# Chunk attention with its weight remainders on VectorE instead of GpSimd

## The chip, the core and the metric

The kernel runs on one core of a Trainium2 chip. The metric is the device time of one execution in microseconds (us); smaller is better. The engines are TensorE (PE, with PEld for its weight loads), VectorE (DVE), ScalarE (ACT), GpSimd (POOL) and SyncE (SP), whose queue issues almost all transfers. Each engine works through its own instructions in the order of the program, and instructions of different engines wait for each other through semaphores.

## The reference

A two-layer trunk over 512 frames of width 1024. Layer 0 is a state-space mixer beside a convolution module; layer 1 is the chunk attention that the change touches; each layer is followed by cross-attention into 256 memory tokens. Layer 1, cut to what matters (chunks of 64 frames, each of which sees itself and the 8 before it; 16 heads of 64):

```
q, k, v, g = jnp.split(h @ w_in, 4, axis=-1)          # h: 512 x 1024, w_in: 1024 x 4096
s = einsum('bqhd,bkhd->bhqk', qc, kc) * scale + bias  # for each chunk, bias by clipped distance
s = where(valid, s, -1e30)
o = einsum('bhqk,bkhd->bqhd', softmax(s), vc)
x = x + (o * silu(g)) @ w_out
```

All products are wanted in near float32 precision.

## The kernel before

**Products in three parts.** Every large matrix product splits both operands into a rounded part (`hi`) and a remainder (`lo`), and sums hi·hi, hi·lo and lo·hi. Activations are split once. A block of weights, 128 x 8 x 128 or 128 x 4 x 256 (1024 numbers per partition), is loaded by SyncE into `raw`, rounded by a ScalarE cast into `whi`, and its remainder `raw - whi` goes into `wlo`. That is `weights`, which calls `split`; the engine of the subtraction is the argument `eng`, and GpSimd where none is given. There are three buffers of `raw`, two of `whi` and three of `wlo`.

**Units as filler.** In chunk attention the 32 weight blocks of queries, keys, gates (24 blocks, `qk_unit`, `g_unit` and `first`) and values (8 blocks, `v_unit`) are worked off by generators that yield after each matmul. The products that need `wlo` stand last in each unit: 16 of 24 matmuls come before them. The class `Filler` hands out so many matmuls between the steps of the attention as the lists `GAPS`, `LEAST` and so on allow; TensorE's order is therefore written out in full and pinned.

**Eight pairs of heads.** The loop over `hp` treats two heads at a time; the text calls them pair 0 to pair 7. For each pair the scores are made in three goes, rows 0 and 1, row 2, and row 3 (a row is 128 queries; row i has 128 (i+1) keys). Behind each go VectorE finds the peak with the bias (`peak`, L1269 to L1272), ScalarE takes the exponential (L1257), VectorE the reciprocal and the scaling (L1259, L1260, recorded as L162: tiles `pe0` to `pe3`, in the profile `pe`). Then TensorE transposes the scaled rows (L84, `transposed`) with filler between, VectorE and ScalarE split each transposed block (`pt`), and the weighting by the values follows in the next pair. The last transpose of the first block needs the scaled row 3 of the first head, `pe` 128x512.

In the same stretch VectorE and ScalarE finish queries and keys (`qk_finish`: `z`, then casts and subtractions, half of these on GpSimd by the table `QE`), gates, values, and the output of the pair before (`output`: two additions into `o`, the gating L157 `o<-o,g`, the cast to `og` on ScalarE and the remainder of `og` on GpSimd). `tz` is a head's bias table, loaded and shifted once for each head (L1235, recorded as L162).

A list scheduler sets the order of VectorE's and ScalarE's instructions by its own estimates; `tc.high_priority()` puts a group ahead of others. Helpers record under their own lines: L153 is `tt`, L157 is `stt`, L162 is `ts` with one operand, L168 the cast in `split`.

Of the kernel before, what the change touches and what calls it, by code (L numbers as in the profile page):

```python
# [18 lines left out]
SEQ = 512  # L19
MEM = 256  # L20
# [24 lines left out]
def kernel(  # L45
# [22 lines left out]
    V, A, G = nc.vector, nc.scalar, nc.gpsimd  # L68
# [43 lines left out]
    def tl(tag, shape=(P, SEQ), dt=F32):  # L112
        pool, n = tags[tag]
        return pool.tile(list(shape), dt, tag=tag, name=nm(tag), bufs=n)

    def rl(tag, shape=(P, SEQ)):
        return tl(tag, shape, F32R)
# [10 lines left out]
    def psum(tag):  # L128
        return pp.tile([P, 512], F32, tag=tag, name=nm("ps_" + tag), bufs=PS[tag])
# [16 lines left out]
    def f(ap):  # L146
        return ap.bitcast(F32)

    def pinned(ins):
        tc.keep_in_program_order(ins)  # L150

    def tt(out, a, b, op, eng=None):
        (eng or V).tensor_tensor(out, a, b, op=op)  # L153
        return out

    def stt(out, a, s, b, op0, op1):
        V.scalar_tensor_tensor(out=out, in0=a, scalar=s, in1=b, op0=op0, op1=op1)  # L157
        return out
# [8 lines left out]
    def split(src, hi, lo, eng=None):  # L167
        A.copy(hi, src)  # L168
        tt(lo, src, f(hi), ALU.subtract, eng or G)
        return hi, lo  # L170

    def weights(src, kt=8, n=P, eng=None, tag="whi"):
        raw = tl("raw", (P, kt, n))
        nc.sync.dma_start(raw, src)
        hi = rl(tag, (P, kt, n))
        lo = rl("wlo", (P, kt, n))
        with tc.high_priority():
            split(raw, hi, lo, eng)
        return hi, lo
# [66 lines left out]
    def gsplit(x, g, hi, lo):  # L246
        A.activation(hi, x, AF.Copy, scale=g)  # L247
        stt(lo, x, g, f(hi), ALU.mult, ALU.subtract)
        return hi, lo
# [11 lines left out]
    def norm_split(gname, goff=0):  # L261
        st = Stats()
        h = []
        with tc.high_priority():
            for i in range(KT):
                h.append(gsplit(x[i], pc(gname, goff + i), rl("h"), rl("h")))
                st.add(x[i])
        return h, st

    def rb_tile(rs):  # L270
        ps = bcast(rs, SEQ)
        t = tl("rb")
        A.copy(t, ps)
        return t
# [446 lines left out]
    for job in LOADS.split():  # L721
        n = int(job[1])
# [12 lines left out]
    with tc.high_priority():  # L735
        for job in ACTS.split():
            n = int(job[1])
# [161 lines left out]
    for sl in range(4):  # L899
        t = tl("uu")  # L900
# [48 lines left out]
    def silu_gate(ps, rb):  # L949
        with tc.high_priority():  # L950
            z = tt(tl("z"), ps, rb, ALU.mult)
            g = tl("g")
            A.activation(g, z, AF.Tanh, scale=0.5)
            stt(g, g, 1.0, z, ALU.add, ALU.mult)
        return g
# [40 lines left out]
    def products(terms):  # L996
        prods = []
        for (ah, al), (bh, bl) in terms:
            prods += [(ah, bh), (ah, bl)]
        return prods + [(al, bh) for (ah, al), (bh, bl) in terms]  # L1000

    def unit(wsrc, act, finish, last=None, tag="whi", cols=slice(0, SEQ)):
        wh, wl = weights(wsrc, tag=tag)
        n = cols.stop - cols.start
        ps = psum("proj")[:, :n]
        prods = products([((wh[:, k, :], wl[:, k, :]), act[k]) for k in range(last or len(act))])
        for i, (a, b) in enumerate(prods):
            pinned(T.matmul(ps, a, b[:, cols], start=(i == 0), stop=(last is None and i == len(prods) - 1)))
            yield 0.2135 * n / SEQ
        finish(ps, wh, wl)  # L1010

    def cross_attention(layer, kv, h, st, w_d, cols=slice(0, SEQ)):
# [4 lines left out]
        def q_unit(hd, e):  # L1017
            def finish(ps, wh, wl):
                hi, lo = rl("q"), rl("q")
                with tc.high_priority():  # L1020
                    split(ps, hi, lo, V)
                qs[hd, e] = (hi, lo)

            return ("q", hd, e), unit(xa_qg_d[layer, 2 * hd + e], h, finish)

        def g_unit(hd, e):
            def finish(ps, wh, wl):
                gs[hd, e] = silu_gate(ps, norm["rb"])

            return ("g", hd, e), unit(xa_qg_d[layer, 8 + 2 * hd + e], h, finish)  # L1030

        def part_unit(i):
            def finish(ps, wh, wl):
                part[i] = (ps, wh, wl)

            return ("r", i), unit(w_d[i], og, finish, last=6, cols=cols)
# [101 lines left out]
    def chunk_attention(h, st, w_d):  # L1138
# [5 lines left out]
        def qk_finish(hp, e):  # L1144
            def finish(ps, wh, wl):
                t = tl("z")
                a, b = rl("qk"), rl("qk")
                u, d = slice(0, 64), slice(64, P)
                with tc.high_priority():
                    if e == 0:  # L1150
                        stt(t, ps, 0.125, norm["rb"], ALU.mult, ALU.mult)
                        split(t[u], a[u], a[d], QE[0])
                        split(t[d], b[d], b[u], QE[1])
                        qs[hp] = (a, b)
                    else:
                        lo = klo[hp % 2]
                        tt(t, ps, norm["rb"], ALU.mult)
                        split(t[u], a[u], lo[0][u], QE[2])
                        split(t[d], b[d], lo[1][d], QE[3])
                        A.copy(a[d], t[u])  # L1160
                        A.copy(b[u], t[d])
                        ks[hp] = (a, b) + lo
            return finish

        def first():
            late = []

            def keep(ps, wh, wl):
                late.append(ps)
            for t in unit(od_qkg_d[0], h, keep):  # L1170
                yield t
            norm["rs"] = st.done()

            klo.extend([(rl("sq"), rl("sq")), (rl("kl"), rl("sa"))])
            for pair in klo:
                for e, t in enumerate(pair):
                    G.memset(f(t[64 * (1 - e):64 * (2 - e)]), 0.0)
            for t in unit(od_qkg_d[1], h, keep):
                yield t
            norm["rb"] = rb_tile(norm["rs"])  # L1180
            for e in range(2):
                qk_finish(0, e)(late[e], None, None)

        def qk_unit(hp, e):
            return ("qk"[e], hp), unit(od_qkg_d[3 * hp + e], h, qk_finish(hp, e))

        def g_unit(hp):
            def finish(ps, wh, wl):
                gs[hp] = silu_gate(ps, norm["rb"])

            return ("g", hp), unit(od_qkg_d[3 * hp + 2], h, finish)

        def v_unit(gr):
            def gen():
                v = []
                pss = [psum("proj") for _ in range(2)]
                outs = [pss[i // 2][:, (i % 2) * MEM:(i % 2 + 1) * MEM] for i in range(NT)]
                for e in range(2):
                    wh, wl = weights(od_v_d[gr, e], kt=4, n=MEM)
                    for low in range(2):  # L1200
                        for t, o in enumerate(outs):
                            ts_ = slice(t * P, (t + 1) * P)
                            for k in range(4):
                                ah, al = h[4 * e + k]
                                for j, (a, b) in enumerate([(ah, wl)] if low else [(ah, wh), (al, wh)]):
                                    pinned(T.matmul(o, a[:, ts_], b[:, k, :],
                                                    start=(e == 0 and low == 0 and t % 2 == 0 and k == 0 and j == 0),
                                                    stop=(e == 1 and low == 1 and t % 2 == 1 and k == 3)))
                                    yield 0.107
                for i in range(NT):  # L1210
                    e = rl("vv", (P, 4, 2, 64))
                    src = outs[i].rearrange("p (a c) -> p a c", a=4)
                    with tc.high_priority():
                        gsplit(src, norm["rs"][:, i:i + 1], e[:, :, 0], e[:, :, 1])
                    v.append(e.rearrange("p a t c -> p a (t c)"))
                vs[gr] = v

            return ("v", gr), gen()
# [7 lines left out]
        def units():  # L1226
            yield ("qk", 0), first()
            for kind, i in UNITS:
                yield {"q": lambda: qk_unit(i, 0), "k": lambda: qk_unit(i, 1), "g": lambda: g_unit(i),
                       "v": lambda: v_unit(i), "r": lambda: part_unit(i)}[kind]()  # L1230
# [127 lines left out]
    h, st = norm_split("xa_g", 0)  # L1358
# [7 lines left out]
    h, st = norm_split("od_g")  # L1366
# [7 lines left out]
    h, st = norm_split("xa_g", 8)  # L1374
# [164 lines left out]
```

## Time and profile before

| | |
|---|---|
| three runs | 998.61, 994.61, 997.92 us; median 997.92 us |
| profiled execution | 994.67 us |
| its span | 992.9 us, so 1.8 us lie around it |
| chunk attention's units and pairs | about 459 to 745 us of the span |

The table of runs is what a later time is compared with. The span is what the profile's rows add up to: from the first to the last instruction of the profiled execution. A time in a row that is marked as a start counts from the span's start.

### The profile page before, as it was taken

The page shows a single profiled execution, that of the slowest core. Times are in us where ns is not written, and L with a number is a line of the kernel's source. Part 1 is how long each engine was busy: PE and PEld are TensorE (multiplying, and loading weights), DVE is VectorE, ACT ScalarE, POOL GpSimd, SP SyncE. Part 2 cuts the span into 40 slices and gives each one's busy share as a digit, 9 for nine tenths or more (in the row PEclk, how much of TensorE's full clock was granted, in tenths as well). Part 3 has the DMA queues.
Part 4 walks back from the last instruction along what each step waited for, and adds up shares of the span by engine and source line. Part 5 has one row for each costly group of instructions (what it writes and reads, how often), then busy time and mean ns, then how long its engine had stood idle before and what let it go on. Part 6 is the DMA issues. An engine that isn't in the chain of part 4 may idle for free.

```text
span 992.9 us, 14232 instructions
## 1 busy us (share of the span) xinstructions
PE 956.0 (96%) x5336; PEld 817.4 (82%) x5336; DVE 565.7 (57%) x1260; ACT 469.2 (47%) x845; POOL 442.3 (45%) x245
## 2 busy tenths in 40 slices
PE   9999999989999999999999999999999999999996
PEld 7788889759888888888787887878878998888895
DVE  7975257874344333452668767787667313333476
ACT  6333445565443434444456655656535543434352
POOL 1022333049676334457444435344327983443241
PEclk9999999999999999999999999999999999999998
DMA  8365656347523222223122222222214453222153
GB/s 290 119 191 180 195 157 191 104 159 229 162 98 91 79 81 69 64 96 107 64 75 75 75 68 92 75 75 75 64 43 138 151 189 107 64 85 76 52 169 107
DMA packets 53621, 113.71 MB, mean 115 GB/s; under 512 B 13233, under 2 KB 24625, under 8 KB 53553
## 3 DMA queue, kind: packets, MB, share of 16 engines
q1 hardware_dynamic: 53408, 112.74, 35.5%
q8 instruction: 42, 0.69, 0.3%
q14 instruction: 27, 0.21, 0.1%
q10 hardware_dynamic: 144, 0.07, 0.0%
HBM read 106.50 MB, written 6.29 MB: 114 GB/s over the span
## 4 chain that ended last, share of the span: by engine, by line
PE 34%; DVE 9%; issue 3%; ACT 2%; DMA 1%; POOL 1%; POOLq 0%; ACTq 0%; DVEq 0%
PE ps_proj L81 27%; PE ps_att L81 2%; PE ps_tr L84 2%; PE ps_acc L81 2%; PE ps_tr L81 1%; DVE pe L162 1%; ACT whi L168 1%; DVE ps_att L1270 1%; DVE tz L162 1%; DVE o L153 1%; DVE h L157 1%; POOL wlo L153 1%; ACT pe L1257 1%; DVE s L1269 1%; DMA mt<-in_memT_dram 1%
## 5 line engine op out<-in xcount | busy, mean ns | idle before, releaser
L153 POOL TENSOR_TENSOR wlo<-raw,whi 128x1024 fp32r<-128x1024 f32 x130 | 317.7, 2448 | 411.1 <-ACT whi L168 366.0
L81 PE MATMUL ps_proj<-h,whi 128*128 128x512 f32 x1184 | 299.4, 397 | 2.4 <-DVE ang L153 2.4
L81 PEld LDWEIGHTS ps_proj<-h,whi 128*128 128x128 f32 x1184 | 217.5, 188 | 47.4 <-issue 5.1
L168 ACT CAST whi<-raw 128x1024 fp32r<-128x1024 f32 x148 | 155.1, 1049 | 191.3 <-PE ps_proj L81 91.8
L81 PE MATMUL ps_proj<-h,wlo 128*128 128x512 f32 x592 | 151.7, 394 | 0.0
L81 PE MATMUL ps_proj<-og,whi 128*128 128x512 f32 (+1 forms) x672 | 135.0, 348 | 0.5 <-DVE og L153 0.5
L81 PEld LDWEIGHTS ps_proj<-h,wlo 128*128 128x128 f32 x592 | 111.0, 189 | 22.7
L81 PEld LDWEIGHTS ps_proj<-og,whi 128*128 128x128 f32 x672 | 107.6, 188 | 17.9 <-DVE og L153 2.0
L81 PE MATMUL ps_proj<-og,wlo 128*128 128x512 f32 (+1 forms) x344 | 73.4, 348 | 0.1
L81 PEld LDWEIGHTS ps_proj<-og,wlo 128*128 128x128 f32 x344 | 56.1, 188 | 8.9 <-POOL wlo L153 0.4
L153 DVE TENSOR_TENSOR pt<-ps_tr,pt 128x512 fp32r<-128x512 f32 (+1 forms) x80 | 39.9, 526 | 32.4 <-ACT pt L168 32.3
L168 ACT CAST pt<-ps_tr 128x512 fp32r<-128x512 f32 (+1 forms) x80 | 34.3, 460 | 49.1 <-PE ps_tr L84 48.8
L162 DVE TENSOR_SCALAR pe<-pe,s 128x256 f32<-128x256 f32 (+3 forms) x96 | 51.2, 555 | 1.4
L1257 ACT ACTIVATE pe<-ps_att,s 128x128 f32<-128x128 f32 (+3 forms) x64 | 33.6, 526 | 36.4 <-DVE s L162 32.5
L153 DVE TENSOR_TENSOR z<-ps_proj,rb 128x512 f32<-128x512 f32 x32 | 22.0, 688 | 46.3 <-PE ps_proj L81 46.2
L153 POOL TENSOR_TENSOR sa<-sa,sq 128x512 f32<-128x512 f32 (+1 forms) x28 | 38.9, 1388 | 18.9 <-ACT sq L228 18.2
L153 DVE TENSOR_TENSOR x<-ps_proj,x 128x512 f32<-128x512 f32 (+1 forms) x38 | 22.9, 603 | 41.7 <-PE ps_proj L81 41.7
L153 DVE TENSOR_TENSOR kv<-ps_proj,kv 128x256 fp32r<-128x256 f32 (+1 forms) x24 | 12.2, 511 | 60.2 <-ACT kv L168 59.3
L157 DVE SCALAR_TENSOR_TENSOR h<-x,par,h 128x512 fp32r<-128x512 f32 x24 | 38.6, 1613 | 13.5 <-ACT h L247 13.5
L84 PE MATMUL ps_tr<-ident,pe 128*128 128x128 f32 x224 | 35.9, 279 | 9.5 <-DVE pe L162 5.0
L81 PEld LDWEIGHTS ps_proj<-x,cw 128*128 128x128 f32 x320 | 39.1, 191 | 5.1 <-DMA cw<-in_cw_dram 3.1
L84 PEld LDWEIGHTS ps_tr<-ident,pe 128*128 128x128 f32 x224 | 27.1, 142 | 18.7 <-DVE pe L162 6.7
(244 smaller groups left out, 1448.3 us busy)
## 6 DMA issues: line engine op xcount, KB each, us to landing
raw<-in_xa_qg_dram SPq DMA_DIRECT2D x32, 512.0 KB, 3.4
raw<-in_od_qkg_dram SPq DMA_DIRECT2D x24, 512.0 KB, 3.5
raw<-in_xa_o_dram SPq DMA_DIRECT2D x22, 512.0 KB, 3.5
cw<-in_cw_dram SPq DMA_DIRECT2D x32, 320.0 KB, 3.6
raw<-in_w_in_dram SPq DMA_DIRECT2D x18, 512.0 KB, 4.3
raw<-in_xa_k_dram SPq DMA_DIRECT2D x16, 512.0 KB, 3.7
raw<-in_xa_v_dram SPq DMA_DIRECT2D x16, 512.0 KB, 3.5
x<-in_xT_dram SPq DMA_DIRECT2D x16, 256.0 KB, 5.0
```

The lines of the kernel that those rows point to most:

```text
L81: return self.keep(nc.tensor.matmul(*args, **kw))
L84: return self.keep(nc.tensor.transpose(*args))
L153: (eng or V).tensor_tensor(out, a, b, op=op)
L157: V.scalar_tensor_tensor(out=out, in0=a, scalar=s, in1=b, op0=op0, op1=op1)
L162: V.tensor_scalar(out=out, in0=in0, scalar1=s1, scalar2=None, op0=op0)
L168: A.copy(hi, src)
L1257: A.activation(st_["pe"][i], ps[:, c:c + n], AF.Exp, bias=nb, accum_out=st_["sums"][:, i:i + 1])
L1269: V.reduce_max(init, ps[:, :nf], axis=AX.X)
L1270: V.tensor_tensor_reduce(out=ps[:, nf:n], in0=ps[:, nf:n], in1=st["tz"][:, MEM - (n - nf):], scale=1.0, scalar=init, op0=ALU.add, op1=ALU. ...
```

## The change

`unit` gets an argument `eng` and hands it to `weights`, and the units of chunk attention's queries, keys, gates and values pass VectorE. The remainders of the output projection's blocks (`part_unit`), those of half the queries and keys (`QE`) and those of `og` stay on GpSimd.

```
-    def unit(wsrc, act, finish, last=None, tag="whi", cols=slice(0, SEQ)):
-        wh, wl = weights(wsrc, tag=tag)
+    def unit(wsrc, act, finish, last=None, tag="whi", cols=slice(0, SEQ), eng=None):
+        wh, wl = weights(wsrc, tag=tag, eng=eng)
...
-            for t in unit(od_qkg_d[0], h, keep):
+            for t in unit(od_qkg_d[0], h, keep, eng=V):
...
-            for t in unit(od_qkg_d[1], h, keep):
+            for t in unit(od_qkg_d[1], h, keep, eng=V):
...
-            return ("qk"[e], hp), unit(od_qkg_d[3 * hp + e], h, qk_finish(hp, e))
+            return ("qk"[e], hp), unit(od_qkg_d[3 * hp + e], h, qk_finish(hp, e), eng=V)
...
-            return ("g", hp), unit(od_qkg_d[3 * hp + 2], h, finish)
+            return ("g", hp), unit(od_qkg_d[3 * hp + 2], h, finish, eng=V)
...
-                    wh, wl = weights(od_v_d[gr, e], kt=4, n=MEM)
+                    wh, wl = weights(od_v_d[gr, e], kt=4, n=MEM, eng=V)
```

The orders of TensorE and SyncE are the same in both programs. GpSimd loses 32 rows, VectorE gains 32, and the scheduler reorders others around them. On VectorE, in pair 2, around the peak and the scaling of row 3 (`s_5302`, `ps_att_5292`: the second head's peak; `pe_1166`: the first head's scaled row; `o_5280`: the output of the pair before; `wlo_5456`: a new remainder; - is before, + is the change):

```order
 L1269 TENSOR_REDUCE s_5302<-ps_att_5292 128x1
-L157 SCALAR_TENSOR_TENSOR o_5280<-o_5280,g_5061 128x512
+L153 TENSOR_TENSOR o_5280<-ps_tr_5211,z_5281 64x512
 L1270 ISA ps_att_5292,s_5152<-ps_att_5292,tz_5149,s_5302 128x256
 L1270 ISA s_5152 128x1
 L1259 RECIPROCAL s_5148<-s_5147 128x1
+L157 SCALAR_TENSOR_TENSOR o_5280<-o_5280,g_5061 128x512
+L153 TENSOR_TENSOR wlo_5456<-raw_5453,whi_5455 128x1024
 L162 TENSOR_SCALAR s_5305<-s_5152 128x1
 L162 TENSOR_SCALAR pe_1166_5307<-pe_1166_5307,s_5148 128x512
```

The gating and the new remainder now stand between the second head's peak and the first head's scaled row. The same happens in pairs 1, 3 and 5.

On ScalarE at the same place (`og_5287`: the cast of the gated output, after which GpSimd forms its remainder; `pe_1167`: the second head's exponential):

```order
 L1257 ACTIVATE pe_1166_5307,s_5147<-ps_att_5291,s_5300 128x512
 L168 CAST whi_5455<-raw_5453 128x1024
+L168 CAST og_5287<-o_5280 128x512
 L1257 ACTIVATE pe_1167_5309,s_5153<-ps_att_5292,s_5305 128x512
-L168 CAST og_5287<-o_5280 128x512
```

The cast of the output moved ahead of the second head's exponential.

On VectorE in pair 4, at the same step (`pe_1346`: the first head's scaled row; `o_6005`, `wlo_6201` as above):

```order
 L1259 RECIPROCAL s_5860<-s_5859 128x1
+L153 TENSOR_TENSOR o_6005<-ps_tr_5935,z_6006 64x512
 L162 TENSOR_SCALAR s_6030<-s_5864 128x1
 L162 TENSOR_SCALAR pe_1346_6032<-pe_1346_6032,s_5860 128x512
+L157 SCALAR_TENSOR_TENSOR o_6005<-o_6005,g_5908 128x512
+L153 TENSOR_TENSOR wlo_6201<-raw_6198,whi_6200 128x1024
```

Here the gating and the remainder went behind the scaled row.

## Rows read from the trace of the kernel before

**Rows 1.** The page: busy time, share of the span, instructions of each engine.
```profile
PE 956.0 (96%) x5336; PEld 817.4 (82%) x5336; DVE 565.7 (57%) x1260; ACT 469.2 (47%) x845; POOL 442.3 (45%) x245
```

**Rows 2.** By stretch: length, busy time of each engine, granted clock, DMA share, GB/s.
```profile
486.60:490.00 3.40, 3.40 (x9) 2.62 (x9) 1.39 (x9) 1.75 (x5) 2.14 (x1) 0.50 0.00 0
510.50:513.90 3.40, 3.40 (x18) 3.40 (x17) 0.00 (x0) 0.00 (x0) 0.36 (x1) 0.50 0.43 154
480.00:720.00 240.00, 227.41 (x1287) 193.84 (x1285) 177.18 (x494) 139.44 (x303) 102.04 (x54) 0.99 0.23 74
```

**Rows 3.** TensorE's waits, 480 to 745: us in total, times, longest.
```profile
PE ps_tr L84 <- DVE pe L162: 5.0, 7, 1.6
PE ps_tr L84 <- DVE pt L153: 4.3, 6, 1.6
PE ps_att L81 <- ACT qk L1160: 1.7, 1, 1.7
```

**Rows 4.** TensorE in order of time: start, us, instruction, [idle before, releaser].
```profile
507.95 0.44 PE L84 MATMUL ps_tr<-ident,pe 128*128 128x128 f32 x2 [0.78 <-DVE pt L153]
509.26 0.33 PE L84 MATMUL ps_tr<-ident,pe 128*128 128x128 f32 x1 [0.87 <-DVE pt L153]
...
536.48 0.66 PE L84 MATMUL ps_tr<-ident,pe 128*128 128x128 f32 x4 [0.28 <-DVE pe L162]
...
543.07 0.33 PE L84 MATMUL ps_tr<-ident,pe 128*128 128x128 f32 x1 [1.65 <-DVE pt L153]
...
569.26 0.66 PE L84 MATMUL ps_tr<-ident,pe 128*128 128x128 f32 x4 [0.58 <-DVE pe L162]
...
600.29 0.65 PE L84 MATMUL ps_tr<-ident,pe 128*128 128x128 f32 x4 [1.58 <-DVE pe L162]
...
631.95 0.66 PE L84 MATMUL ps_tr<-ident,pe 128*128 128x128 f32 x4 [1.55 <-DVE pe L162]
```

**Rows 5.** Tile wlo, the whole span: times, duration ns min/median/max, first and last start.
```profile
L153 POOL TENSOR_TENSOR wlo<-raw,whi x130: 2343/2406/3125, 57.0 to 972.8; 128x1024 fp32r<-128x1024 f32 x130
...
L153 DVE TENSOR_TENSOR wlo<-raw,whi x18: 1206/1220/2086, 15.1 to 977.3; 128x1024 fp32r<-128x1024 f32 x18
```

**Rows 6.** VectorE's groups by form, 420 to 745: times | busy us, mean ns | idle before.
```profile
L162 DVE TENSOR_SCALAR pe<-pe,s 128x384 f32<-128x384 f32 x16 | 15.9, 993 | 0.2
L162 DVE TENSOR_SCALAR tz<-tz,par 128x256 f32<-128x256 f32 x16 | 14.9, 934 | 1.2 <-DMA tz<-in_toep_dram 1.2
L162 DVE TENSOR_SCALAR pe<-pe,s 128x512 f32<-128x512 f32 x16 | 14.6, 913 | 0.2
...
L157 DVE SCALAR_TENSOR_TENSOR o<-o,g 128x512 f32<-128x512 f32 x8 | 5.5, 685 | 0.0
```

**Rows 7.** VectorE in pairs 2 and 3: start, us, instruction, [idle before].
```profile
560.64 0.42 DVE L162 TENSOR_SCALAR pe<-pe,s 128x384 f32<-128x384 f32 x1
561.95 0.16 DVE L1259 RECIPROCAL s<-s 128x1 f32<-128x1 f32 x1 [0.89 <-ACT pe L1257]
...
562.62 1.43 DVE L162 TENSOR_SCALAR pe<-pe,s 128x384 f32<-128x384 f32 x1
...
568.07 0.49 DVE L1270 CUSTOM_DVE_ANT_0 ps_att<-ps_att,tz,s 128x256 f32<-128x256 f32 x1
...
568.73 0.48 DVE L162 TENSOR_SCALAR pe<-pe,s 128x512 f32<-128x512 f32 x1
569.12 0.35 DVE L162 TENSOR_SCALAR tz<-tz,par 128x256 f32<-128x256 f32 x1
...
592.60 1.89 DVE L162 TENSOR_SCALAR pe<-pe,s 128x384 f32<-128x384 f32 x1
```

**Rows 8.** GpSimd in pair 2, in order of time.
```profile
561.42 2.41 POOL L153 TENSOR_TENSOR wlo<-raw,whi 128x1024 fp32r<-128x1024 f32 x1 [6.33 <-ACT whi L168]
563.92 1.29 POOL L153 TENSOR_TENSOR qk<-z,qk 64x512 fp32r<-64x512 f32 x1
...
571.68 1.49 POOL L153 TENSOR_TENSOR og<-o,og 128x512 fp32r<-128x512 f32 x1
```

## The prediction

> **What bounds the kernel now.** I read the page first, then TensorE's waits in the stretch of the change, then VectorE around each wait. TensorE is busy for 96% of the span, VectorE for 57%, GpSimd for 45% [rows 1]: only what TensorE waits for can be won or lost. In 480 to 720 it is busy for 227.4 of 240 us [rows 2], so 12.6 us are open there. Most of them are waits of the transposes, 5.0 us for scaled rows (`pe`) and 4.3 us for split blocks (`pt`), both VectorE's; another 1.7 us is the start of pair 0 [rows 3]. No row has TensorE waiting for a `wlo` in this stretch. Almost every pair has one such wait, 0.28 to 1.65 us, at the same step: the last transpose of the first block needs the first head's scaled row 3 [rows 4].
>
> The clock matters too. Twice in the stretch the granted clock is 0.50 for 3.40 us, so the 1.2 GHz level [rows 2]. Each time TensorE had just waited: 1.7 us at the start of pair 0 [rows 3] before the first, 0.78 and 0.87 us close together before the second. Single waits of 1.65, 1.58 and 1.55 us cost no clock [rows 4]. In 3.40 us at half the clock TensorE does 1.7 us of work, so one fall costs 1.7 us.
>
> **The change part by part.**
>
> *Removed from GpSimd, added to VectorE.* 24 blocks of queries, keys and gates and 8 of values, 32 instructions. On GpSimd one takes 2.41 us, on VectorE 1.22 us [rows 5]: 77 us leave GpSimd, 39 us come to VectorE. GpSimd's were hidden behind 16 matmuls of each unit (the filler's own figure for one, 0.2135 us in L1009, makes 3.4 us at least); VectorE's are ready even sooner once they start, so the remainders as such cost TensorE nothing.
>
> *What VectorE gets back.* A scaling of 128x384 takes 0.42 us when GpSimd is idle, but 1.43 us from 562.62, ending at 564.05, just behind GpSimd's `wlo`, which ended at 563.83 [rows 7, 8]. So VectorE is held until GpSimd's instruction is over. Against the undisturbed 0.42, 0.35 and 0.48 us [rows 7] the 16 scalings of 384, the 16 of `tz` and the 16 of 512 average 0.99, 0.93 and 0.91 us [rows 6]: (0.57 + 0.58 + 0.43) x 16 = 25 us of holding. Some is due to GpSimd's other work, which stays, so about 20 us come back. VectorE's busy time in 480 to 720 goes from 177 to some 190 of 240 us; it does not become the bound on average. What counts is the order at the waits.
>
> *Pair 2, step by step.* Until the second head's peak (568.07 before [rows 7]) VectorE gains one remainder, 1.14 us from start to start (successive instructions overlap by 0.08 to 0.09 us, as 568.73, 0.48 long, and 569.12 show). Of its 0.89 us of idleness before the second 384-scaling 0.54 us goes; I leave 0.35 us, an estimate, for the cast that the remainder needs. It has the gating moved behind the peak (0.60 us from start to start, 0.68 us long [rows 6]). The scaling is held once more, now by GpSimd's remainder of the query (1.29 us [rows 8]), and gains only 0.25 us. Sum: 1.14 - 0.54 - 0.60 - 0.25, about -0.3 us: the peak starts at 567.8. Then, by the new order, the gating (0.60), the new remainder (1.2) and only then the first head's scaled row. Meanwhile ScalarE casts the gated output, and GpSimd's remainder of `og` (1.3 to 1.5 us, [rows 8]) is ready and queued when VectorE's remainder ends. I take it that it goes first and holds the scaled row for 1.3 us. The row then ends at 567.8 + 0.5 + 0.6 + 1.2 + 1.3 + 0.25 = 571.65 instead of 568.73 + 0.48 = 569.21 [rows 7]: **+2.45 us**. TensorE waits 3.0 instead of 0.58 us [rows 4], and nothing later in this pair waited that could give it back.
>
> *The hold by `og`* is nowhere in the rows at this very instruction. Its bounds are 0 (if the scaled row gets in first) and 1.5 us; I take 1.3, since the row that it is nearest to is the scaling held to GpSimd's end [rows 7, 8]. It occurs in pairs 1, 2, 3 and 5. The Trainium skill, SBUF — State Buffer, "Who interferes with whom", lets the later of the two wait for the whole instruction, and that also for VectorE instructions with two SBUF inputs, such as the new remainders; by it the whole 1.3 us stands in all four pairs (5.2 us), without it the sum would be 5.2 us less. The scaling row agrees; for the new remainders no row here shows it.
>
> *The other pairs.* Pair 3 has the same order, but its 384-scaling had been held longer (1.89 us [rows 7]), so its peak comes about 0.9 us earlier: +1.8 us, the wait becomes 1.6 + 1.8 = 3.4 us. Pair 5 has pair 2's order, waits as briefly and has, by my count, 0.3 us less to get back: +2.75 us. In pair 1 a `z` stands before the scaled row as well; the wait of 0.28 us grows to about 3.0 us, but the later one of 1.65 us [rows 4] and a short one ahead of it then find their blocks done, which gives back about 2 us: +0.6 us net. In pair 4 the scaled row stays ahead of gating and remainder, and its wait of 1.55 us [rows 4] goes: -1.55 us. Pair 0 waited 1.65 us for `pt` behind two held scalings; two remainders come in there, so I take half: -0.8 us. Pair 6: +0.3 us, pair 7: 0, its order is unchanged. The start of pair 0 (rb, `z`) gains 0.4 us, the mean holding of one scaling in rows 6, since one short instruction there is held. In the stretch before, 459 to 480, remainders stand between the residual's additions and the splits of `h`; a block of `h` comes some 0.5 us later, and the first unit reads it last: 0, at most +0.5 us if that cover is gone.
>
> Sum of waits: 2.45 + 1.8 + 2.75 + 0.6 - 1.55 - 0.8 + 0.3 - 0.4 = **+5.1 us**.
>
> *The clock.* Four waits of about 3 us are longer than any of before, and 1.7 us was enough once. I count three falls of the four, and one of before's two gone: 2 x 1.7 = **+3.4 us**. Bounds: -3.4 us (none new, both old gone) and +6.8 us (four new).
>
> Sum: +8.5 us. The profiled execution took 994.67 us, which makes 1003.2; the median of the runs is 997.92, 3.25 us above it, and with the same addition I predict **1006 us**.
>
> **Rivals.**
>
> *A, the forecast:* slower, the scaled row 3 waits behind gating, remainder and `og`. For it: the order in four pairs and rows 7.
>
> *B, faster: the relief wins.* VectorE's freed holding pulls the second peak forward by more than the 3.1 us (0.6 + 1.2 + 1.3) that now stand between it and the scaled row. That decides at 3.1 us a pair; in pair 2 I count 0.3, in pair 3 0.9. If it did, all 9.3 us of transposes' waits [rows 3] and both clock falls would go: 997.9 - 9.3 - 3.4 = 985; half of it gives 992. Against it: only 20 us come back over eight pairs, 2.5 us each, while each gets 4.9 us of remainders. The Trainium skill, GPSIMD Engine Reference, "Engine selection", speaks for it: elementwise work belongs on VectorE, GpSimd being about twice as slow with two inputs. The ratio of rows 5, 1.97, agrees; taken alone the rule would give the 992 of this rival.
>
> *C, no change.* The hold by `og` does not occur (5.1 - 5.2 = 0 us) and the clock falls as often as before: 998; or it occurs and the later waits in pairs 2, 3 and 5 shrink, as in pair 1: +2 to +4, 1000 to 1002. For it: pair 1's rows.
>
> *D, VectorE becomes the bound.* If none of the holding came back, it would be busy 177 + 39 = 216 of 240 us, and waits for `z` and `pt` would appear at each pair; at one more wait of 1.6 us in each of eight pairs, on top of the forecast, 1019 us. Against it: the held rows are held by just what leaves.
>
> **How the numbers follow.** Chances: A 0.55, B 0.14, C 0.27, D 0.04. A measurement of this kernel tells about 0.5% (5 us) from no change. Slower by over 0.5% is A and D less A's small end (1003 and below), but some of C lies above: 0.57. Within 0.5%: 0.29. Faster: 0.14. The range: from 5.1 - 5.2 - 3.4 = -3.5 us, 994.5, to 5.1 + 6.8 + 3 x 1.2 for larger holds in pairs 0, 6 and 7 = 15.5 us, 1013.5; below lies most of B, above D. A's own range is 1001 to 1012.
>
> **What would show it.** VectorE's `wlo` of 1.2 us, 32 more; scalings of `pe` and `tz` near 0.42, 0.48 and 0.35 us except beside GpSimd's short work. TensorE's wait for `pe` rises from 5.0 to about 14 us, in pairs 1, 2, 3 and 5, each some 3 us; in pair 4 it is gone; that for `pt` falls from 4.3 to below 1.5 us. The clock row has three or four half-clock stretches of 3.4 us after such waits. The prediction is wrong if the scaled row 3 of pair 2 ends within 1 us of its old distance from the second peak, if `og` never holds it, or if waits of 3 us leave the clock at full.

## The result, and the profile after

| | median, us | runs, us | ratio to before, 95% interval |
|---|---|---|---|
| before | 997.68 | 991.24 to 999.40 | |
| with the change | 1001.17 | 999.46 to 1006.98 | 1.0057, 1.0032 to 1.0082 |

The change makes the kernel slower by 0.3 to 0.8%. The ratio agrees with the means of the ten runs of each, 996.65 and 1002.33 us; the medians lie only 3.5 us apart. The profiled execution took 1001.4 us for a span of 999.6, 6.7 us more than the span before. One execution each of e1 and e4 below took some 1914.6 us, twice as long as the others, and stands in no median and no ratio.

The page, busy time of each engine, to set beside [rows 1]:

```profile
PE 958.5 (96%) x5336; PEld 821.4 (82%) x5336; DVE 585.1 (59%) x1292; ACT 470.0 (47%) x845; POOL 365.0 (37%) x213
```

GpSimd lost 77 us. VectorE gained 19, not 39. Some 15 us were paid with time in which GpSimd had held it (see the relief below), so its rows sum to 24 us more; the other 5 us are overlap of successive rows, which busy time counts once. TensorE's waits, 480 to 745 (total, times, longest), which answer to [rows 3]:

```profile
PE ps_tr L84 <- DVE pe L162: 15.5, 6, 3.6
PE ps_att L81 <- ACT qk L1160: 1.3, 1, 1.3
...
PE ps_tr L84 <- DVE pt L153: 0.3, 1, 0.3
```

Waits for split blocks went from 4.3 to 0.3 us, those for scaled rows from 5.0 to 15.5. TensorE in order of time (start, us, instruction, idle before), which answers to [rows 4]: the wait in pair 0 has shrunk, pairs 1, 2, 3 and 5 wait over 3 us, and pair 4's wait is gone.

```profile
506.66 0.33 PE L84 MATMUL ps_tr<-ident,pe 128*128 128x128 f32 x1 [0.28 <-DVE pt L153]
...
535.44 0.66 PE L84 MATMUL ps_tr<-ident,pe 128*128 128x128 f32 x4 [3.38 <-DVE pe L162]
...
569.96 0.99 PE L84 MATMUL ps_tr<-ident,pe 128*128 128x128 f32 x4 [3.11 <-DVE pe L162]
...
604.49 1.11 PE L84 MATMUL ps_tr<-ident,pe 128*128 128x128 f32 x4 [3.54 <-DVE pe L162]
...
668.60 0.66 PE L84 MATMUL ps_tr<-ident,pe 128*128 128x128 f32 x4 [3.60 <-DVE pe L162]
```

The stretches behind these four waits, and that of before's second fall (length, busy time of each engine, granted clock, DMA share, GB/s): the clock is at half behind all four. The last line is the stretch in which it had fallen before [rows 2]; in the change it is at full there, and also from 506.7 to 510.1, where the products of before's second fall now run.

```profile
536.00:539.40 3.40, 3.40 (x10) 2.63 (x10) 3.30 (x6) 1.53 (x4) 0.78 (x1) 0.50 0.21 82
570.10:573.50 3.40, 3.40 (x17) 3.40 (x17) 1.99 (x6) 1.07 (x2) 0.00 (x0) 0.51 0.31 116
604.30:607.70 3.40, 3.21 (x10) 2.73 (x11) 3.05 (x8) 1.48 (x3) 0.00 (x0) 0.50 0.36 137
669.10:672.50 3.40, 3.40 (x11) 2.66 (x10) 2.30 (x5) 1.50 (x4) 0.00 (x0) 0.50 0.19 78
510.50:513.90 3.40, 3.40 (x31) 3.40 (x31) 1.26 (x3) 0.94 (x5) 0.00 (x0) 1.00 0.22 92
```

Pair 2 on VectorE:

```profile
566.10 0.49 DVE L1270 CUSTOM_DVE_ANT_0 ps_att<-ps_att,tz,s 128x256 f32<-128x256 f32 x1
...
566.69 0.67 DVE L157 SCALAR_TENSOR_TENSOR o<-o,g 128x512 f32<-128x512 f32 x1
567.28 1.22 DVE L153 TENSOR_TENSOR wlo<-raw,whi 128x1024 fp32r<-128x1024 f32 x1
...
568.48 1.42 DVE L162 TENSOR_SCALAR pe<-pe,s 128x512 f32<-128x512 f32 x1
```

and on GpSimd:

```profile
568.16 1.46 POOL L153 TENSOR_TENSOR og<-o,og 128x512 fp32r<-128x512 f32 x1 [4.72 <-ACT og L168]
```

The second peak, the gating and the remainder come first, and then a scaled row of 1.42 instead of 0.48 us, which ends (569.90) just behind GpSimd's work on `og` (569.62). TensorE goes on at 569.96.

The lengths of the pairs, each from its first score product on TensorE to that of the next (pair 7 to one and the same product of the output projection in both), with the waits in it (the sum of TensorE's idle times):

| us | pair 0 | 1 | 2 | 3 | 4 | 5 | 6 | 7 |
|---|---|---|---|---|---|---|---|---|
| before: length | 35.42 | 32.21 | 30.53 | 31.41 | 31.97 | 30.25 | 31.69 | 42.46 |
| its waits | 1.91 | 2.33 | 0.58 | 1.63 | 1.81 | 0.64 | 0.96 | 1.44 |
| change: length | 32.17 | 34.43 | 34.69 | 34.25 | 29.80 | 34.40 | 32.36 | 41.94 |
| its waits | 0.53 | 3.38 | 3.14 | 3.54 | 0.02 | 3.60 | 2.03 | 1.09 |

Waits grow by 6.0 us. For the rest, TensorE's order is the same in both programs, so its starts can be compared instruction by instruction. Over each of the four half-clock stretches the change falls back by 1.5 to 1.6 us, 6.2 us together; over before's second one it gains 1.6 us. Another 2.5 us come back in small pieces, nearly all at transposes that had started up to 0.22 us late in the kernel before, waits too short to be listed. Pair 0 began 0.9 us sooner (483.62 against 484.52): 0.4 us of this is its first wait (1.7 to 1.3 us), and 0.5 us were there before the first unit. Behind the pairs 0.5 us came back. Sum: 6.0 + 6.2 - 1.6 - 2.5 - 0.9 - 0.5 = 6.7 us.

### The profile page after: what moved, and what is told of

Same layout as the page of the kernel before. It is cut to its first block, busy times and chain, and to the rows that moved or that the text cites. A ratio compares the mean times of both kernels' runs of the same rounds, so it can differ in the third digit from the quotient of the medians.

```text
span 999.6 us, 14227 instructions
## 1 busy us (share of the span) xinstructions
PE 958.5 (96%) x5336; PEld 821.4 (82%) x5336; DVE 585.1 (59%) x1292; ACT 470.0 (47%) x845; POOL 365.0 (37%) x213
## 4 chain that ended last, share of the span: by engine, by line
PE 35%; DVE 8%; issue 3%; ACT 2%; DMA 1%; POOL 1%; POOLq 0%; ACTq 0%; DVEq 0%
PE ps_proj L81 28%; PE ps_att L81 2%; PE ps_tr L84 2%; PE ps_acc L81 2%; PE ps_tr L81 1%; DVE pe L162 1%; DVE wlo L153 1%; ACT whi L168 1%; DVE h L157 1%; POOL wlo L153 1%; DVE o L153 1%; DVE ps_att L1270 1%; DVE s L1269 1%; DMA mt<-in_memT_dram 1%; DMA tz<-in_toep_dram 0%
## 5 line engine op out<-in xcount | busy, mean ns | idle before, releaser
L153 POOL TENSOR_TENSOR wlo<-raw,whi 128x1024 fp32r<-128x1024 f32 x98 | 239.7, 2451 | 305.0 <-ACT whi L168 280.7
L81 PE MATMUL ps_proj<-h,whi 128*128 128x512 f32 x1184 | 304.2, 401 | 2.9 <-DVE ang L153 2.9
L81 PEld LDWEIGHTS ps_proj<-h,whi 128*128 128x128 f32 x1184 | 220.9, 191 | 49.2 <-issue 5.6
L153 DVE TENSOR_TENSOR wlo<-raw,whi 128x1024 fp32r<-128x1024 f32 x50 | 62.3, 1247 | 43.6 <-ACT whi L168 43.2
L84 PE MATMUL ps_tr<-ident,pe 128*128 128x128 f32 x224 | 34.9, 279 | 15.8 <-DVE pe L162 15.5
L162 DVE TENSOR_SCALAR pe<-pe,s 128x256 f32<-128x256 f32 (+3 forms) x96 | 43.8, 479 | 1.3
```

Source lines behind the costliest of these rows:

```text
L81: return self.keep(nc.tensor.matmul(*args, **kw))
L84: return self.keep(nc.tensor.transpose(*args))
L162: V.tensor_scalar(out=out, in0=in0, scalar1=s1, scalar2=None, op0=op0)
```

## The experiments

The theory on trial: the loss is the place of the remainder (and of the gating and the hold by `og`) ahead of the first head's scaled row 3. Rivals: VectorE's added load, whatever its place; no hold by `og`; no worth in the relief. All versions start from the change. Each was measured beside runs of the kernel before, whose medians were 997.63 (e1 to e4), 996.99 (e5 to e8) and 996.22 us (e9 to e12); the ratios are taken from the runs, not from the medians.

| kernel | what | median, us | ratio to before, 95% interval |
|---|---|---|---|
| e1 | remainders without priority | 989.66 | 0.9912, 0.9887 to 0.9937 |
| e2 | remainders pinned behind the row | 985.25 | 0.9876, 0.9848 to 0.9905 |
| e3 | `og`'s remainder left out | 996.59 | 0.9993, 0.9972 to 1.0013 |
| e4 | units' remainders left out | 984.06 | 0.9848, 0.9824 to 0.9871 |
| e5 | `og`'s remainder on VectorE | 995.35 | 0.9985, 0.9961 to 1.0010 |
| e6 | gates' remainders on GpSimd | 1003.53 | 1.0053, 1.0031 to 1.0076 |
| e7 | as e2, not the last values' unit | 985.24 | 0.9872, 0.9843 to 0.9901 |
| e9 | e6, the output's work pinned | 1004.11 | 1.0076, 1.0048 to 1.0103 |
| e10 | the change, the output's work pinned | 1004.88 | 1.0087, 1.0057 to 1.0118 |
| e11 | gates' remainders alone moved | 995.18 | 0.9991, 0.9966 to 1.0016 |
| e12 | as e7, `og`'s remainder on VectorE | 990.35 | 0.9937, 0.9909 to 0.9965 |

What decides is best seen in one table: from the start of the first head's exponential of row 3 (ScalarE) to the start of the scaled row (VectorE), that row's duration, and TensorE's wait for it, all in us, read from the traces.

| | pair 1 | pair 2 | pair 3 | pair 5 |
|---|---|---|---|---|
| before | 1.40, 0.48, 0.28 | 1.40, 0.48, 0.58 | 1.40, 0.48, 1.58 | 1.40, 0.48, 0.59 |
| change | 3.96, 0.83, 3.38 | 3.09, 1.42, 3.11 | 3.36, 1.43, 3.54 | 3.36, 1.42, 3.60 |
| e1 | 2.23, 0.48, 1.28 | 1.95, 0.48, 1.02 | 2.22, 0.48, 1.44 | 2.23, 0.48, 1.51 |
| e2 | 1.40, 0.48, 0 | 1.12, 0.48, 0 | 1.40, 0.48, 0.10 | 1.40, 0.48, 0.23 |
| e3 | 3.96, 0.48, 3.02 | 3.08, 0.48, 2.18 | 3.36, 0.48, 2.60 | 3.36, 0.48, 2.64 |
| e6 | 1.40, 0.48, 0.33 | 1.95, 2.52, 3.06 | 2.23, 2.51, 3.54 | 2.23, 2.51, 3.60 |

**e1**

```
-            split(raw, hi, lo, eng)
+            A.copy(hi, raw)
...
+        if eng is V and late:
+            tt(lo, raw, f(hi), ALU.subtract, V)
```

> The change, with the VectorE remainders of chunk attention's units put into the list without priority: in pairs 1, 2, 3 and 5 VectorE's order is then peak, gating, first head's scaled row 3, remainder. The same 39 us of remainders stay on VectorE and off GpSimd. Theory A (the place in the queue is the loss): remainder and the hold by GpSimd's og work leave the way of the scaled row, 1.2 + 0.9 us less in each of the four pairs; their waits of 3.1 to 3.6 us fall to about 1.0 to 1.4 us, the four clock falls behind them go, and the span is 4 x (2.1 + 1.2) = 13 us below that of the change: 986 to 991 us. Rival D (VectorE's load is the loss): the work is as much as before, so waits for pe or pt come up elsewhere, 998 to 1003 us. Rival (the relief is small and the later place costs the units' own wlo): TensorE waits for wlo show up, 994 to 998 us.

Measured: 989.66 us. The subtraction now stands outside the group with priority. In pair 2 the remainder follows the row, and no `og` work meets it:

```profile
567.35 0.67 DVE L157 SCALAR_TENSOR_TENSOR o<-o,g 128x512 f32<-128x512 f32 x1
...
568.00 0.48 DVE L162 TENSOR_SCALAR pe<-pe,s 128x512 f32<-128x512 f32 x1
568.39 1.22 DVE L153 TENSOR_TENSOR wlo<-raw,whi 128x1024 fp32r<-128x1024 f32 x1
```

The four waits are 1.0 to 1.5 us and no clock fall follows them. One fall is left in these pairs (granted clock 0.50 from 540.2 to 543.6), behind a wait of 1.74 us for a split block in pair 1. The same load in another place is some 12 us faster: the load is not the loss.

**e2**

```
+            with tc.issue_after(row3[-1]) if row3 and eng is V else nullcontext():
+                split(raw, hi, lo, eng)
...
+                        if i == 3 and st_ is sts[0]:
+                            row3[:] = [ins.ins]
```

> The change, with every VectorE remainder that is written behind row 3's scores pinned behind the first head's scaled row 3; the gating goes ahead of the second peak, as in the kernel before. Two remainders then stand in a row between the first and the second head's scaled row. Theory A: the waits of pairs 1, 2, 3 and 5 for pe fall to at most those of before (0.3 to 1.6 us), no clock falls behind them, 985 to 990 us. Rival D (load): the 2.4 us of remainders only move the wait to the next step, the second head's row or the split blocks pt, which rise by 2 us a pair: 998 to 1003 us.

Measured: 985.25 us. VectorE in pair 2:

```profile
561.30 0.68 DVE L157 SCALAR_TENSOR_TENSOR o<-o,g 128x512 f32<-128x512 f32 x1
561.90 0.49 DVE L1276 CUSTOM_DVE_ANT_0 ps_att<-ps_att,tz,s 128x256 f32<-128x256 f32 x1
...
562.55 0.48 DVE L1263 TENSOR_SCALAR pe<-pe,s 128x512 f32<-128x512 f32 x1
562.95 2.35 DVE L153 TENSOR_TENSOR wlo<-raw,whi 128x1024 fp32r<-128x1024 f32 x2
```

Two remainders stand behind the row, one of which had stood ahead of the peaks. TensorE's waits, 480 to 745:

```profile
PE ps_tr L84 <- DVE pt L153: 1.9, 3, 1.6
PE ps_proj L81 <- DVE wlo L153: 1.8, 1, 1.8
...
PE ps_tr L84 <- DVE pe L1263: 0.6, 2, 0.3
```

Waits for rows are down to 0.6 us, those for blocks do not rise, and the one new wait, for a remainder in pair 6, is the price of the pin. Rival D is out for this load.

**e3**

```
-            og[hp] = split(o, rl("og"), rl("og"), V if hp == 7 else G)
+                hi = rl("og")
+                A.copy(hi, o)
+                og[hp] = (hi, hi)
```

> The change without the remainder of og on GpSimd in pairs 0 to 6: the rounded part is used in its place, so that part of the computation is left out; TensorE's instructions are as many as before, and VectorE's order in pairs 1, 2, 3 and 5 is that of the change. Theory A with the hold: the scaled row 3 takes 0.48 us again, not 1.42, in pairs 2, 3 and 5 and 0.35 us less in pair 1, so the waits of 3.1 to 3.6 us fall by 0.9, 0.9, 0.9 and 0.35 us, the sum is 3.2 us; waits of 2.2 us still cost the clock: 997 to 998.5 us, and 994 if they don't. Rival (no hold by og; the row is long for another reason): the row stays at 1.4 us and the time at 1001 us.

Measured: 996.59 us, just below the 997 of the theory with the hold. The row takes 0.48 us in all four pairs (table), so the hold was real: 0.35 us in pair 1, 0.94 in the others, 3.2 us of waits. A wait of 1.63 us in pair 6 went as well, but not because of the hold: the load of `tz`, for which VectorE had sat idle there, landed 2.5 us after its issue instead of 4.8. Why it was quicker stays open.

**e4 and e8**

```
+            if eng is V and zero:
+                A.copy(hi, raw)
+                return hi, zero[0][:, :, :n] if kt == 8 else ...
             split(raw, hi, lo, eng)
```

> The 32 remainders of queries, keys, gates and values are left out on both engines; a block of zeros stands in their place, so those products are left out of the sum, though TensorE runs as many matmuls. VectorE's order is that of the kernel before. This is the relief without the added work. Theory A: VectorE's held instructions shrink (scalings to 0.42 to 0.55 us beside GpSimd's short work), about 20 us of holding go, the transposes' waits of 9.3 us in the kernel before fall to 2 to 4 us and one or two clock falls go: 985 to 991 us. Rival (the holding was off the path): waits stay near 9 us and the time within 994 to 998 us.

> The relief alone once more, with the 32 remainders left out on both engines, for its waits: if its 984 us comes from VectorE being free of the holding, the transposes' waits of 9.3 us are down to below 2 us in the stretch from 480 to 745 us; if it comes from elsewhere (later stretches, the clock), they stay at 4 us or more.

Measured: 984.06 us, and 982.09 in the single run of e8 (the same kernel as e4), whose trace is shown. TensorE's waits in e8, 480 to 745:

```profile
PE ps_tr L84 <- DVE pt L153: 1.3, 2, 0.8
...
PE ps_tr L84 <- DVE pe L162: 0.6, 2, 0.3
```

The transposes wait for 1.9 us where they waited for 9.3 [rows 3], and before's second clock fall is gone. GpSimd's remainders had thus cost the kernel before some 13 us. TensorE waited for none of them in this stretch [rows 3]; the waits that went are nearly all for VectorE. Beside e2's 985.25 us (and the ratios 0.9848 and 0.9876) the work that VectorE does in their place costs 1 to 3 us.

**e5**

```
-            og[hp] = split(o, rl("og"), rl("og"), V if hp == 7 else G)
+            og[hp] = split(o, rl("og"), rl("og"), V)
```

> The change with the remainder of og on VectorE in all pairs; VectorE's order in pairs 1, 2, 3 and 5 is peak, gating, remainder, first head's scaled row, remainder of og. All products are formed. If the hold by GpSimd's og work is a real cost of the change, the scaled row takes 0.48 us and the waits of pairs 2, 3 and 5 fall by 0.9 us as without that remainder; VectorE does 7 x 0.7 = 4.8 us more behind the row, where the second head's row has some us of cover: 995 to 998 us. Rival D (load): the 4.8 us come back as waits for the second head's row or pt: 999 to 1002 us.

Measured: 995.35 us; the waits are those of e3 (3.02, 2.18, 2.59, 2.65 us). Without the hold the median is 5 to 6 us lower, whichever way it is taken off. The hold itself is 3.2 us of this. The rest is the wait in pair 6, shorter by 1.6 us in e3 and by 0.4 in e5, and clock falls that did not come: in the profiled executions one in e3 (pair 1) and three in e5 (pairs 3 and 5, and the start of pair 0, where nothing was changed).

**e6**

```
-            return ("qk"[e], hp), unit(od_qkg_d[3 * hp + e], h, qk_finish(hp, e), eng=V)
+            return ("qk"[e], hp), unit(od_qkg_d[3 * hp + e], h, qk_finish(hp, e), eng=G if (hp, e) == (3, 1) else V)
...
-            return ("g", hp), unit(od_qkg_d[3 * hp + 2], h, finish, eng=V)
+            return ("g", hp), unit(od_qkg_d[3 * hp + 2], h, finish, eng=G)
```

> The change with the remainders of the gates' units, and of pair 3's keys, back on GpSimd; queries, the other keys and values stay on VectorE. These are the units whose remainder stood ahead of the scaled row in pairs 1, 2, 3 and 5; in pairs 2, 3 and 5 the gating still stands ahead of it, in pair 1 nothing does. Theory A: the waits of these pairs fall to 0.5 to 1.5 us, as with the remainders put in without priority, the clock falls behind them go and most of the relief is kept: 989 to 993 us. Rival (VectorE is held by the 2.4 us of a gate's remainder on GpSimd just at the scaled row): waits of 1.5 to 2.5 us stay in these pairs, 994 to 999 us. Rival D (load): 23 of 32 remainders stay, so 3/4 of the loss stays: 997 to 1000 us.

Measured: 1003.53 us. This is the clearest miss: the mechanism of the rival (VectorE held by a gate's remainder), with waits of 3.06 to 3.60 us, even longer than it gave, and a time above all three ranges. Pair 2, VectorE and then GpSimd:

```profile
567.30 2.52 DVE L162 TENSOR_SCALAR pe<-pe,s 128x512 f32<-128x512 f32 x1
```

```profile
567.19 2.34 POOL L153 TENSOR_TENSOR wlo<-raw,whi 128x1024 fp32r<-128x1024 f32 x1 [3.79 <-issue]
```

The cast of the gate's block stands right behind the first exponential on ScalarE, so GpSimd's remainder starts some 1.8 us after that exponential. In the kernel before the row started 1.40 us after it and ended at 569.21 [rows 7]; GpSimd's remainder there:

```profile
569.17 2.57 POOL L153 TENSOR_TENSOR wlo<-raw,whi 128x1024 fp32r<-128x1024 f32 x1 [3.96 <-DVE s L162]
```

The row was through just in time. Here the row comes 1.95 us after it, 0.11 us behind the remainder, and is held for 2 us. The remainder costs as much ahead of the row on GpSimd as on VectorE. The Trainium skill, SBUF — State Buffer, "Who interferes with whom", says that the later of the two waits for the whole instruction; the 2.52 us agree.

**e7**

```
+                    wh, wl = weights(od_v_d[gr, e], kt=4, n=MEM, eng=V, pin=gr < 3)
```

> The remainders pinned behind the first head's scaled row 3, but not those of the last values' unit, whose first remainder TensorE waited 1.8 us for in pair 6 when it was pinned. In pair 6 VectorE's order is then that of the change, with the scaling of the second head's row 2 ahead of the scaled row 3. If that wait is all there is to win, 982 to 984 us; if a wait for pe of about 1.0 to 1.6 us takes its place, as in the change and without priority, 984 to 986 us and no difference to the pinned version.

Measured: 985.24 us. The wait for the remainder went and one for a scaled row, 0.77 us, came in pair 6: no difference to e2.

**e9 and e10**

```
+                        with tc.issue_after(outs[e]) if i == 3 and outs else nullcontext():
+                            nbs.append(peak(st_, i, ps[:, c:c + n]))
```

> The version with the gates' remainders (and pair 3's keys) on GpSimd, and now VectorE's order of the kernel before around row 3: the second addition into o ahead of the first head's peak, the gating ahead of the second head's. In the version without this order the row was held for 2.52 us by the gate's remainder on GpSimd, which started at 567.19, the row at 567.30; from the first head's exponential to the row were 1.95 us, in the kernel before 1.41 us. Refined theory (the row races with the remainder, whose cast stands right behind the exponential, and 0.6 us of output work between the peaks lose the race): the row starts before GpSimd and takes 0.48 us, the waits of pairs 2, 3 and 5 fall from 3.1 to 3.6 us to below 0.8 us, 986 to 991 us. Rival (GpSimd holds it anyway, or load): waits above 2 us stay, 997 to 1003 us.

> The change, all remainders of the units on VectorE, with the same two instructions of the output put ahead of the peaks; the gate's remainder still stands ahead of the scaled row in pairs 2 to 5, pair 1 has none there. This tells the 0.6 us of the output's work apart from the remainder and the hold. If the remainder's 1.2 us and the hold by og are the main part: waits of 1.5 to 2.6 us in pairs 2 to 5, pair 4's among them, some clock falls, 993 to 998 us. If the output's place alone made the loss: waits below 1 us, 986 to 990 us.

Measured: 1004.11 and 1004.88 us. e9 came out 1 us above the range of its rival, e10 7 us above both of its ranges, and neither tells what it was made for. The pin put the whole gating between the first head's peak and the negation that its exponential waits for; the kernel before has the gating behind that negation. So the exponential came later, and in ScalarE's order of e9 the cast of the gate's block now stood ahead of it (pair 2):

```profile
567.71 1.05 ACT L168 CAST whi<-raw 128x1024 fp32r<-128x1024 f32 x1 [2.21 <-PE ps_proj L81]
568.78 0.69 ACT L1260 ACTIVATE pe<-ps_att,s 128x512 f32<-128x512 f32 x1
```

GpSimd's remainder then ran ahead of the row again, which took 1.74 us. In e10 the waits are 3.44, 2.30, 2.71 and 3.65 us in pairs 1, 2, 3 and 5, and pair 4, whose order now has the remainder ahead of the row too, waits for 2.86. How much of the change's loss is the 0.6 us of the output's work between the peaks stays open, but for e1's rows, in which that work alone stands in front (1.95 to 2.23 against 1.40 us).

**e11**

```
-            return ("g", hp), unit(od_qkg_d[3 * hp + 2], h, finish)
+            return ("g", hp), unit(od_qkg_d[3 * hp + 2], h, finish, eng=V)
```

(here against the kernel before)

> One part alone: only the 8 gates' remainders on VectorE, queries, keys and values on GpSimd as before. VectorE's order has the scaled row ahead of the gate's remainder in pairs 2 to 6, and the gating where it was before, except in pair 1. A quarter of the work moves, and the one that held the second head's row for 2 us in the kernel before. Theory A: no new wait, the relief in part: the waits of 1.5 us in pairs 3 and 5 fall by half, 990 to 995 us. Rival (the relief needs all of GpSimd's remainders gone, since those of queries and keys hold the scalings before the peak): no difference, 995 to 999 us. Rival D: 1/4 of the change's loss, 998 to 999 us.

Measured: 995.18 us, not told apart from before. The waits of pairs 2, 3 and 5 stayed as they were (0.56, 1.58 and 0.59 us): this part alone gives no relief there. The relief lies ahead of the exponential: from the end of row 3's scores on TensorE to the first head's exponential are 3.75 and 4.51 us in pairs 2 and 3 of the kernel before, 3.00 and 3.03 in e2. In pair 1 the gating slipped ahead of the row and the row into a remainder on GpSimd (538.37 to 541.02):

```profile
538.81 2.51 DVE L162 TENSOR_SCALAR pe<-pe,s 128x512 f32<-128x512 f32 x1
```

The wait there went from 0.28 to 3.31 us. This is e6's race again, lost in one pair.

**e12**

The edits of e5 and e7 together.

> The pinned version without the last values' unit, with the remainder of og on VectorE as well, where it stands behind the second head's reciprocal. If the hold by og still costs something where remainders stand behind the row (VectorE's second remainder took 1.88 us beside it in pair 1): 982 to 984 us, and pair 1's wait of 1.6 us for pt shrinks. If VectorE's added 0.7 us a pair delays the second head's row: 985 to 988 us.

Measured: 990.35 us, 5 us more than e7 and above both ranges. TensorE waits for split blocks three times as long as in e2 (480 to 745):

```profile
PE ps_tr L84 <- DVE pt L153: 5.8, 5, 2.3
```

VectorE in pair 1 of e12:

```profile
538.52 1.70 DVE L153 TENSOR_TENSOR og<-o,og 128x512 fp32r<-128x512 f32 x1
...
540.97 0.48 DVE L1263 TENSOR_SCALAR pe<-pe,s 128x512 f32<-128x512 f32 x1
541.37 1.15 DVE L153 TENSOR_TENSOR pt<-ps_tr,pt 128x512 fp32r<-128x512 f32 x2
```

and of e2:

```profile
535.09 0.67 DVE L153 TENSOR_TENSOR pt<-ps_tr,pt 128x512 fp32r<-128x512 f32 x1
...
536.82 0.49 DVE L1263 TENSOR_SCALAR pe<-pe,s 128x512 f32<-128x512 f32 x1
537.22 0.55 DVE L153 TENSOR_TENSOR pt<-ps_tr,pt 128x384 fp32r<-128x384 f32 x1
```

The second head's row is not late: it starts 5.78 us behind the first head's here and 5.73 in e2. But the remainder of `og` took the place in which the first block `pt` had been split, and both blocks now follow the row. So another 0.7 us in front of the blocks (1.7 in pair 1, beside GpSimd's `qk`), behind two remainders, does cost. Where the limit lies was not tried.

## Why the prediction was right

The forecast was slower, 1006 us; measured were 1001.17, a little inside the small end of A's own range. The mechanism held: the scaled row 3 waits behind the gating, the remainder and GpSimd's `og` in pairs 1, 2, 3 and 5, and four clock falls follow. Some terms were mis-sized, and two errors cancel. One reading was off: at that step the waits before are 0.21 to 1.58 us; the 1.65 us counted with them is a wait for a split block [rows 4]. No term rests on it.

**The relief.** Forecast 20 us of holding given back. VectorE's groups, 420 to 745, which answer to [rows 6]:

```profile
L162 DVE TENSOR_SCALAR pe<-pe,s 128x384 f32<-128x384 f32 x16 | 12.2, 767 | 0.1
L162 DVE TENSOR_SCALAR pe<-pe,s 128x512 f32<-128x512 f32 x16 | 10.9, 681 | 0.2
L162 DVE TENSOR_SCALAR tz<-tz,par 128x256 f32<-128x256 f32 x16 | 7.1, 468 | 1.4 <-DMA tz<-in_toep_dram 1.4
```

(0.993 - 0.767 + 0.913 - 0.681 + 0.934 - 0.468) x 16 = 14.8 us. The other 10 of the 25 us stayed, mostly beside GpSimd's `og` and `qk`.

**Pair 2, step by step.** Forecast +2.45 us, from the second peak's start to the row's end 3.85 us; measured 566.10 to 569.90, 3.80 us, and the wait went from 0.58 to 3.11, +2.53. The hold was 0.94 us and the whole row 1.42, where 1.3 + 0.25 was put. In pair 1, where a `z` lies between, the hold was 0.35; in all four pairs it makes 3.2 us, not 5.2.

**The other pairs**, by the table of waits: pair 1 +1.05 (forecast +0.6), pair 3 +1.91 (+1.8), pair 4 -1.79 (-1.55), pair 5 +2.96 (+2.75), pair 0 -1.38 (-0.8), the start -0.4 (-0.4). Pair 6 is the worst: its wait for the row went from 0.21 to 1.63 us, where +0.3 was put in all. The shift of `tz` moved ahead of the row, and VectorE sat idle for its load, which landed 4.8 us after its issue (VectorE in pair 6):

```profile
701.42 0.35 DVE L162 TENSOR_SCALAR tz<-tz,par 128x256 f32<-128x256 f32 x1 [1.35 <-DMA tz<-in_toep_dram]
701.69 0.48 DVE L162 TENSOR_SCALAR pe<-pe,s 128x512 f32<-128x512 f32 x1
```

In e3 the shift stands at the same place, its load landed after 2.5 us, and neither VectorE nor TensorE waited.

Waits in sum +5.6 us with the start, against +5.1.

**The clock.** Forecast three falls of four and one old one gone, 1.7 us each; there were four, and the old one went. Each was worth 1.5 to 1.6 us by TensorE's starts, so the price was nearly right and the number one too low: 6.2 - 1.6 = +4.6 us against +3.4.

**The rest.** The profiled execution grew by 6.7, not 8.5 us, although waits and clock came to more than was forecast. The sum had no term for the short waits of the transposes: 2.5 us of them went with the relief. That they make up for the fourth fall and the longer waits (1.7 us together) is luck. Another 0.5 us came ahead of the units and 0.5 behind the pairs: 5.6 + 4.6 - 2.5 - 0.5 - 0.5 = 6.7 us. The median grew by only 3.5: before's profiled execution lay 3 us below its median, the change's 0.2 us above. Adding the difference of single executions to a median was the weakest step. At 440 us, ahead of the units, the profiled executions of the versions lie 1.2 us ahead of the kernel before (e7) to 4.6 us behind it (e12, with 10.2 us at half clock between 100 and 165 us, where the kernel before has none).

**The rivals.** B gave 985 us if all waits of the transposes and both falls went. The relief for that was there (e4), and with the row ahead of the new work the time came: 985.25 in e2. That the number is the same is partly luck, since 2.5 us of those waits and the fall at the start of pair 0 stayed in e2. In the change the second peak came forward by 0.14 us against TensorE's first transposes (568.07 to 568.19 before, 566.10 to 566.36 after), not by the 3.1 that B needed. The Trainium skill, GPSIMD Engine Reference, "Engine selection", sends elementwise work with two inputs to VectorE; e2 bears that out by 12 us, the change itself does not, since the rule says nothing of where such work queues. C in its second form gave 1000 to 1002 us, where the measured time lies, so the time alone does not tell it from A; the trace does. C's gains in later waits came in pair 1, and only some 0.5 us each of short ones in pairs 3 and 5, while the waits and the falls that A counts are there. C without the hold is e3: no change in time, though with three of the four falls. D is refuted by e2; e12 shows that more load in front of the blocks would cost.

## What to carry to other kernels

Work that moves to another engine should be ranked there by what waits for it: these remainders had slack in every pair but one (pair 6 in e2) and, at high priority, stood ahead of a row that had none; pinned behind it, the same move turned +0.6% into -1.2%. Read the time from the producer of the critical instruction to its start, pair by pair; it shows the loss before the waits are summed. Where two engines hold each other, a step that slips by 0.5 us can cost 2, as in e6, so changes to the order there are to be read from the trace and not from the sum of durations.

## What the runs showed of the hardware that was not expected

The length of a wait does not settle whether the clock falls. e3 and e5 have the same four waits to 0.01 us (3.02, 2.18, 2.6 and 2.65 us in pairs 1, 2, 3 and 5). The stretches behind them in e3:

```profile
535.60:539.00 3.40, 3.40 (x17) 2.90 (x18) 2.99 (x7) 2.35 (x6) 1.40 (x1) 1.00 0.37 145
568.40:571.80 3.40, 3.40 (x19) 3.40 (x18) 1.41 (x3) 0.45 (x2) 0.00 (x0) 0.51 0.37 134
602.50:605.90 3.40, 3.40 (x10) 2.63 (x9) 2.53 (x4) 2.47 (x4) 1.27 (x1) 0.50 0.22 89
664.00:667.40 3.40, 3.34 (x10) 2.86 (x11) 2.21 (x6) 1.49 (x4) 0.00 (x0) 0.51 0.44 154
```

and in e5:

```profile
534.80:538.20 3.40, 3.40 (x10) 2.70 (x9) 3.30 (x7) 1.93 (x5) 1.20 (x1) 0.51 0.31 127
568.90:572.30 3.40, 3.40 (x18) 3.40 (x18) 1.57 (x4) 0.31 (x1) 0.00 (x0) 0.50 0.35 134
601.40:604.80 3.40, 3.38 (x17) 2.88 (x18) 3.40 (x8) 2.73 (x7) 0.74 (x1) 1.00 0.48 154
662.80:666.20 3.40, 3.39 (x17) 2.88 (x18) 3.20 (x8) 2.21 (x6) 0.20 (x1) 1.00 0.47 154
```

The wait of 3.02 us left the clock at 2.4 GHz in e3 and cost it in e5; those of 2.6 us did the reverse. Shorter waits differ in the same way: in pair 1, 1.58 us left the clock at full in e2, and behind 1.57 us it was at half in e7 (536.7 to 540.1). The wait of 1.3 us at the start of pair 0 was followed by a fall in the change and in e1, e2, e3, e6, e8 and e10, and by none in e5, e7, e9 and e12. So a clock term that is worked out from the length of waits has to be given as a range.

A remainder on VectorE, with its two inputs, is held as well: in e2's pair 1 one that started 0.49 us behind GpSimd's remainder of `og` took 1.88 us instead of 1.22. The hold also goes the other way: GpSimd's remainder of `og` took 1.99 us in e2's pair 2, where VectorE formed remainders at the same time, and 1.30 us in its pair 6.
